# Linear attention in a hybrid encoder layer: pairs by values in quarters of the TensorE array, gate logits as one float32r product

## The chip, the cores and the metric

The kernel runs on one core of a Trainium2 chip, in one launch. The metric is the device time of an execution in microseconds (us). TensorE, VectorE, ScalarE, GpSimd and SyncE are the engines of the core; PE, DVE, ACT, POOL and SP in the profile's lines. PEld is TensorE's weight load.

## The reference, cut to what matters

Two layers (DEPTH = 2) on a sequence of 256 positions of width 2048, all in float32. Each layer projects its input to the operands of three mixers, runs them, gates their outputs with SiLU, and maps them back with one output projection, a residual and a LayerNorm. The change touches the second mixer, a gated linear attention (GLA) with 4 heads, keys of 64 and values of 128, in chunks of 64 positions:

```python
gate_logit = (b_lr @ gate_w + gate_b).astype(jnp.float32)     # (256,16) @ (16,256)
log_g = jax.nn.log_sigmoid(gate_logit) / GATE_TAU
...
def step(state, inp):                                         # one chunk of 64 positions
    qc, kc, vc, gc = inp
    b = jnp.cumsum(gc, axis=1)
    decay = jnp.exp(-jnp.abs(b[:, :, None] - b[:, None, :]))
    attn = jnp.einsum('bihd,bjhd,bijhd->bhij', qc, kc, decay)
    o_intra = jnp.einsum('bhij,bjhv->bihv', attn, vc)
    o_inter = jnp.einsum('bihd,bhdv->bihv', qc * jnp.exp(b), state)
    b_last = b[:, -1]
    k_dec = kc * jnp.exp(b_last[:, None] - b)
    new_state = jnp.exp(b_last)[..., None] * state + jnp.einsum('bjhd,bjhv->bhdv', k_dec, vc)
    return new_state, o_intra + o_inter
...
o_b = o_b * lax.rsqrt(jnp.mean(jnp.square(o_b), axis=-1, keepdims=True) + RMS_EPS) * gla_norm_g
```

`attn` is called the pairs here: one 64 by 64 matrix for each head and chunk. `o_intra` is pairs by values, `o_inter` the product with the state of the chunks before.

## The kernel before, in words

**Main stream.** Nearly all of TensorE's work is the weight products of the projections. A load brings a block of weights (512 KB, or 388 KB in the stage that makes the values, `w388`) into a `raw` tile. ScalarE rounds it to float32r, the high part `wh` (L200), and VectorE subtracts to get the low part `wl` (L207). Three float32r products, high by high, low by high and high by low, stand for one float32 product: `stationary` (weights held in the array, x streams) and `moving` (x held, weights stream) issue them; all matmuls are issued at L77. There are four `raw`, four `wh` and three `wl` buffers, and `take` prepares the high part three loads and the low part two loads ahead.

**Side work.** The mixers are Python generators. After each load that is used, `tick` lets one of at most two active generators, the first in the list that is due, issue its next step; `yield n` says in how many ticks it is due again. The order of TensorE and SyncE is the order in which the program issues; a planner orders the instructions of VectorE, ScalarE and GpSimd by a simulated timeline and by priority, and the weight casts and subtracts have a high priority. Side steps take PSUM banks from a list of four (4 to 7) with `banks(n)` and give them back with `release`, in the order of issue.

**GLA before the change.** `gla_inputs` (L356) loads `gate_w` (16 x 256) into rows 0 to 15 of `gw`, a float32 tile whose other rows are zero. `gla` (L364) then runs these steps:

- The 16 low-rank columns are transposed (L372) and copied by VectorE to rows 0 to 15 of `lrT` (L373). Two ticks later two float32 products of `gw` by `lrT` (L378), 256 columns each, give the gate logits; ScalarE adds the bias (L381).
- The decays are built in visits over levels of distance, and the pairs are put together from masked products (L447, L465, L467), in quarters of the array: 64 rows by 64 columns. `pairs[par]` holds, for heads of parity `par`, four groups g = 2t + b (t: half of the sequence, b: head pair); rows 0 to 63 belong to the even chunk of t, rows 64 to 127 to the odd one.
- The last visit also makes the products for the chunk states (L457), and VectorE sums up the states `st` (L472, L475).
- ScalarE copies the pairs into `attn` (L489), whose tiles have two 64 by 64 blocks on the diagonal and zeros elsewhere (zeroed once, L756). Eight float32 products over the full array (L500) give pairs by values for both chunks of a t at once, and twelve products in quarters (L509) add the state part into the same PSUM region.
- ScalarE copies the two banks to `on` (L512), squares are summed (L516), the RMS factor is applied (L522), and after four more ticks `on` is transposed (L528) and ScalarE writes it, scaled by the norm's gain, to `yraw` (L530).

A float32 product appears in the profile as two matmul rows (two passes), a float32r product as one.

In layer 0 the first attention head (`a_head`) starts while GLA is at its last visit; its first step makes scores in one bank, and VectorE reads them at L542.

Of the kernel before, what the change touches and what calls it, by code (L numbers as in the profile page):

```python
# [8 lines left out]
F32 = mybir.dt.float32  # L9
F32R = mybir.dt.float32r  # L10
I32 = mybir.dt.int32
U8 = mybir.dt.uint8
AF = mybir.ActivationFunctionType
ALU = mybir.AluOpType
AX = mybir.AxisListType

P = 128
D = 2048
T = 256
L = 2  # L20
CH = 64
# [22 lines left out]
def hybrid_trunk_kernel(  # L44
# [7 lines left out]
    pe, dve, act, pool, sp = nc.tensor, nc.vector, nc.scalar, nc.gpsimd, nc.sync  # L52
# [4 lines left out]
    def enter(name, bufs=1, **kw):  # L57
        return ctx.enter_context(tc.tile_pool(name=name, bufs=bufs, **kw))

    cst = enter("cst")  # L60
    per = enter("per")
# [6 lines left out]
    ps = psp.tile([P, 8, 512], F32, name="ps")  # L68
# [3 lines left out]
    def nm(s):  # L72
        uid[0] += 1
        return f"{s}_{uid[0]}"

    def mm(o, l, r, start, stop):
        pe.matmul(o, l, r, start=start, stop=stop, skip_group_check=True)  # L77

    def scratch(shape, dtype=F32):
        return sc.tile(shape, dtype, name=nm("sc"), tag="sc")  # L80

    def small(shape, tag, bufs=1):
        return sm.tile(shape, F32, name=nm(tag), tag=tag, bufs=bufs)
# [30 lines left out]
    def banks(n):  # L114
        while len(free) < n:
            yield 1
        return [free.pop(0) for _ in range(n)]

    def release(*bs):
        free.extend(bs)  # L120
# [183 lines left out]
    def ws_group(l, after=None, first=None):  # L304
        for half in range(2):
            a = pair() if half or first is None else first
            for p in range(4):
                w = take()
                for j in range(4):
                    stationary(a, [v[:, j] for v in w], xq[l][p], j, p == j == 0, p == j == 3)  # L310
                if after:
                    after(half, p)
                if p == 3:
                    v = ps[:, a:a + 2].rearrange("p b (h t) -> p b h t", h=2)
                    yield half * 2, v[:, :, 0], v[:, :, 1]
                tick()
# [39 lines left out]
    def gla_inputs(l):  # L356
        gb = small([P, 2], "gb")
        ng = small([P, 1], "ng")
        pool.dma_start(gw[0:16], gate_w[l])
        pool.dma_start(gb, gate_b[l])  # L360
        pool.dma_start(ng, norm_g[l])
        return gb, ng

    def gla(gb, ng, gq, gk, asv, yraw):  # L364
        gqf = gq.rearrange("p b t -> p (b t)")
        gkf = gk.rearrange("p b t -> p (b t)")
        pairs = [hd.tile([P, 4, CH], F32, name=nm("pairs"), tag=f"pairs{par}") for par in range(2)]
        chunks = lambda a: a.rearrange("p (g c) -> p g c", c=CH)

        pt, = yield from banks(1)  # L370
        for t in range(2):
            pe.transpose(ps[:16, pt, t * P:(t + 1) * P], asv[:, t, 0:16], ident)  # L372
        dve.tensor_copy(lrT[0:16], ps[:16, pt, :T])  # L373
        release(pt)
        yield 2
        pl, = yield from banks(1)
# [44 lines left out]
        qe = hd.tile([P, 512], F32, name=nm("qe"), tag="qe")  # L421
# [6 lines left out]
        st = hd.tile([P, 3, 2, P], F32, name=nm("st"), tag="st")  # L428
        for v, levels in enumerate(VISITS):
            last = v == len(VISITS) - 1  # L430
            if v == 0:
                pt, = yield from banks(1)
# [6 lines left out]
            for i, (lev, (kl, ql)) in enumerate(zip(levels, ready)):  # L439
                o = 256 if last else i * 256  # L440
                for t in range(2):
                    for b in range(2):
                        for half in range(2):
                            for par in range(2):
                                rs = slice(par * 64, par * 64 + 64)
# [3 lines left out]
            if last:  # L449
                kv = (pb[2], pb[1])  # L450
                for c in (0, 1, 2):
                    rs = slice((c % 2) * 64, (c % 2) * 64 + 64)
                    t = c // 2
                    for b in range(2):
                        for par in range(2):
                            h = 2 * b + par
# [3 lines left out]
            for i, lev in enumerate(levels):  # L460
                o = 256 if last else i * 256
# [16 lines left out]
            if not last:  # L478
# [4 lines left out]
                    ready.append(decayed(dd))  # L483
                    yield 1
                yield 1
        for par in range(2):
            for half in range(2):
                hs = slice(half * CH, (half + 1) * CH)
                act.copy(attn[par][hs, :, hs], pairs[par][hs])  # L489
        yield 2  # L490

        on = [scratch([P, 4, P]) for _ in range(2)]
        ms = small([P, 8], "ms")
        sq = small([P, P], "sq")
        po = yield from banks(2)
        for par in range(2):
            for t in range(2):
                for b in range(2):
                    h = 2 * b + par
                    mm(ps[:, po[par], (t * 2 + b) * P:(t * 2 + b + 1) * P], attn[par][:, t * 2 + b],  # L500
                       asv[:, t, 16 + h * P:16 + (h + 1) * P], t == b == 0, False)
        for odd, even in ((1, 2), (3, None)):
            for b in range(2):
                for c in (odd, even):
                    if c is not None:
                        for par in range(2):
                            rs = slice(par * 64, par * 64 + 64)
                            g = (c // 2) * 2 + b
                            mm(ps[(c % 2) * 64:(c % 2) * 64 + 64, po[par], g * P:(g + 1) * P],  # L509
                               qe[rs, b * T + c * CH:b * T + (c + 1) * CH], st[rs, c - 1, b], False, True)  # L510
        for par in range(2):
            act.copy(on[par], ps[:, po[par]].rearrange("p (g c) -> p g c", c=P))  # L512
        release(*po)
        for par in range(2):
            for g in range(4):
                act.activation(sq, on[par][:, g], AF.Square, scale=1.0 / math.sqrt(P),  # L516
# [7 lines left out]
        for par in range(2):  # L524
            pt, = yield from banks(1)
            for t in range(2):
                for b in range(2):
                    pe.transpose(ps[:, pt, b * T + t * P:b * T + (t + 1) * P], on[par][:, t * 2 + b], ident)  # L528
            for b in range(2):
                act.activation(yraw[:, 2 * b + par], ps[:, pt, b * T:(b + 1) * T], AF.Copy, scale=ng[:, 0:1])  # L530
            release(pt)


# [171 lines left out]
    eye = cst.tile([P, CH], F32, name="eye")  # L705
    lnt = cst.tile([P, 2, 16], F32, name="lnt")
    lng = cst.tile([P, P], F32, name="lng")
    gw = cst.tile([P, 256], F32, name="gw")
    lrT = cst.tile([P, 256], F32, name="lrT")
    attn = [per.tile([P, 4, P], F32, name=f"attn{par}") for par in range(2)]  # L710

    plan()
    begin()
# [1 line left out]
    for l in range(L):  # L715
# [7 lines left out]
        for s in range(16):  # L723
            value = s in (0, 1) or (s % 2 == 1 and s < 15)
            p = (s if s < 2 else s // 2 + 1) if value else (s - 2) // 2 if s < 15 else 7
# [22 lines left out]
        yraw = [per.tile([P, 4, T], F32, name=nm("yr"), tag=f"yr{i}") for i in range(4)]  # L748
# [1 line left out]
        gk = hd.tile([P, 2, T], F32, name=nm("gk"), tag="gk")  # L750
        free[:] = []
        if l == 0:
            pool.memset(gw, 0.0)
            pool.memset(lrT, 0.0)
            for a in attn:
                pool.memset(a, 0.0)  # L756
        for i, a, b in ws_group(l, None, 4):
            total(gk if i else gq, a, b, 1.0 if i else 0.125)
        gp = gla_inputs(l)
        if l == 0:  # L760
            sp.dma_start(ident, ident_d)
# [9 lines left out]
        asv = per.tile([P, 2, 1552], F32, name=nm("asv"), tag="asv")  # L771
# [5 lines left out]
        def heads():  # L777
            t = hd.tile([P, 4, T], F32, name=nm("qk"), tag="qk", bufs=4)
            for i, a, b in ws_group(l):
                total(t[:, i:i + 2], a, b)  # L780
            return t
# [13 lines left out]
        load_bias(0)  # L795
        load_bias(1)
        gens = [[gla(*gp, gq, gk, asv, yraw[0])]]
        waiting.extend(gens[0])
        for half in range(2):
            values(2 + half)  # L800
            q, k = heads(), heads()
            gens.append([a_head(half * 4 + h, load_bias, bias, q[:, h], k[:, h], asv, yraw[1 + half][:, h]) for h in range(4)])
            waiting.extend(gens[-1])
        q = [hd.tile([P, 4, T], F32R, name=nm("mq"), tag="qk", bufs=4) for _ in range(2)]
# [158 lines left out]
```

## Time and profile before

| | |
|---|---|
| median of 3 runs | 933.64 us (933.53 to 934.63) |
| profiled execution, own time | 933.71 us |
| its span, first to last instruction | 931.9 us |
| mean granted TensorE clock | 0.998 |
| busy: PE, PEld, DVE, ACT, POOL | 923.4, 812.0, 587.3, 502.0, 16.5 us |
| matmul rows of pairs by values (asv,attn) | 32, two layers of 16 |
| matmul rows of the state part (st,qe) | 48, two layers of 24 |
| matmul rows of the gate logits (lrT,gw) | 8, two layers of 4 |

In a line of a group, the tile left of the arrow is written from those on the right; of a matmul these are the streamed operand first and the one held in the array second. "128*128" or "64*64" is the part of the array that is used, then follow the streamed shape and the count. In a line of the timeline the first number is the start, the second the time from the first start to the last end. Matmuls overlap, so the distance between starts tells what one costs, not its duration.

### The profile page before, as it was taken

The numbers are of one execution on the slowest core, as the hardware profiler recorded it, in microseconds if no ns is written. First come the engines' busy times: TensorE is split into PE (matmuls) and PEld (weight loads), VectorE is DVE, ScalarE is ACT, GpSimd is POOL, SyncE is SP. The second block draws the span as 40 slices with busy tenths as digits, with TensorE's granted clock in tenths as the row PEclk, the third lists the DMA queues.
The fourth block names the chain that finished last, engine by engine and source line by source line (L and its number), as shares of the span: only waits on it lengthen the run. The fifth ranks groups of instructions, "written<-read, shape, count | busy, mean of one in ns | idle before, by whom it ended". The sixth has DMA issues, their size and how long they took to land.

```text
span 931.9 us, 14245 instructions
## 1 busy us (share of the span) xinstructions
PE 923.4 (99%) x5530; PEld 812.0 (87%) x5530; DVE 587.3 (63%) x779; ACT 502.0 (54%) x721; POOL 16.5 (2%) x38
## 2 busy tenths in 40 slices
PE   9999999999999999999999999999999999999997
PEld 6889998998888888888888899889988888888875
DVE  5574487655566666555589645964655666675566
ACT  5564484474456665443468446746644566563440
POOL 1000000000000010000000000000000000100000
PEclk9999999999999999999999999999999999999999
DMA  8867755455545467566666666654655455765642
GB/s 294 283 216 273 209 193 173 147 183 180 196 160 168 171 196 224 192 200 186 203 223 182 187 189 190 201 166 151 196 180 180 164 171 181 220 199 191 198 164 90
DMA packets 58451, 178.72 MB, mean 192 GB/s; under 512 B 6352, under 2 KB 9488, under 8 KB 58128
## 3 DMA queue, kind: packets, MB, share of 16 engines
q1 hardware_dynamic: 56560, 173.05, 57.0%
q0 software_dynamic: 1536, 4.24, 2.0%
q8 instruction: 43, 0.70, 0.3%
q10 hardware_dynamic: 288, 0.52, 0.2%
q14 instruction: 24, 0.20, 0.1%
HBM read 175.70 MB, written 2.10 MB: 191 GB/s over the span
## 4 chain that ended last, share of the span: by engine, by line
PE 96%; DMA 1%; DVE 1%; SPq 0%; issue 0%; ACT 0%; ACTq 0%; DVEq 0%
PE ps L77 95%; DMA room<-w 1%; DMA raw<-w 1%; PE ps L559 1%; DVE wl L207 0%; PE ps L655 0%; PE ps L597 0%; SPq L272 0%; PE ps L528 0%; SPq L267 0%; ACT res L687 0%; ACT wh L200 0%; PE ps L435 0%; DVE res L619 0%; PE ps L372 0%
## 5 line engine op out<-in xcount | busy, mean ns | idle before, releaser
L207 DVE TENSOR_TENSOR wl<-raw,wh 128x1024 fp32r<-128x1024 f32 (+1 forms) x313 | 365.9, 1170 | 273.5 <-PE ps L77 208.2
L200 ACT CAST wh<-raw 128x1024 fp32r<-128x1024 f32 (+1 forms) x313 | 314.7, 1007 | 321.1 <-PE ps L77 226.6
L77 PE MATMUL ps<-x,wh 128*128 128x512 f32 x1408 | 448.8, 400 | 0.1
L77 PEld LDWEIGHTS ps<-x,wl 128*128 128x128 f32 x1408 | 264.4, 188 | 63.2 <-DVE wl L207 1.0
L77 PE MATMUL ps<-wh,x 128*128 128x512 f32 (+1 forms) x1112 | 319.2, 368 | 0.0
L77 PE MATMUL ps<-x,wl 128*128 128x256 f32 x1408 | 277.4, 278 | 0.5 <-DVE wl L207 0.5
L77 PEld LDWEIGHTS ps<-wh,x 128*128 128x128 f32 x1112 | 204.7, 188 | 23.9 <-issue 0.7
L77 PEld LDWEIGHTS ps<-x,wh 128*128 128x128 f32 x1408 | 216.5, 189 | 2.4 <-ACT wh L200 0.5
L77 PE MATMUL ps<-wl,x 128*128 128x512 f32 (+1 forms) x556 | 204.5, 368 | 1.1 <-DVE wl L207 1.1
L77 PEld LDWEIGHTS ps<-wl,x 128*128 128x128 f32 x556 | 104.5, 188 | 14.5 <-DVE wl L207 1.9
L550 ACT ACTIVATE sc<-sc,mx 128x128 f32<-128x128 f32 (+1 forms) x32 | 14.3, 448 | 19.8 <-DVE mx L548 19.8
L338 DVE SCALAR_TENSOR_TENSOR sz<-ps,sz 128x512 f32<-128x512 f32 x24 | 16.4, 689 | 2.3 <-ACT sz L337 0.3
L619 DVE SCALAR_TENSOR_TENSOR res<-res,ps 128x512 f32<-128x512 f32 x16 | 10.9, 683 | 8.0 <-PE ps L77 8.0
L337 ACT ACTIVATE sz<-ps 128x512 f32<-128x512 f32 x24 | 14.2, 593 | 2.0 <-DVE x L342 1.3
L77 PE MATMUL ps<-w,x 128*128 128x512 f32 (+1 forms) x72 | 14.3, 357 | 0.0
L77 PEld LDWEIGHTS ps<-w,x 128*128 128x128 f32 x72 | 12.0, 189 | 2.2
L406 ACT ACTIVATE sc<-sc 128x512 f32<-128x512 f32 x12 | 7.6, 633 | 11.6 <-DVE sc L404 11.6
L831 DVE TENSOR_TENSOR yr<-sz,yr 128x512 f32<-128x512 f32 x16 | 11.0, 687 | 4.2 <-ACT sz L829 4.2
L829 ACT ACTIVATE sz<-sz 128x512 f32<-128x512 f32 x16 | 10.1, 633 | 6.1 <-DVE sz L338 6.0
L77 PE MATMUL ps<-qk,qk 128*128 128x128 f32 (+1 forms) x64 | 13.1, 327 | 0.0
L77 PE MATMUL ps<-sc,asv 128*128 128x256 f32 (+1 forms) x64 | 13.0, 326 | 0.0
L342 DVE TENSOR_TENSOR x<-yr,x 128x512 fp32r<-128x512 f32 x16 | 10.7, 688 | 3.2 <-ACT x L341 3.1
(171 smaller groups left out, 515.1 us busy)
## 6 DMA issues: line engine op xcount, KB each, us to landing
raw<-w SPq DMA_DIRECT2D x252, 512.0 KB, 3.6
raw<-w SPq DMA_DIRECT2D x64, 388.0 KB, 3.1
bias<-relw SPq DMA_DIRECT2D x16, 192.0 KB, 4.0
res<-xT SPq DMA_DIRECT2D x4, 512.0 KB, 6.6
res<-xn SPq DMA_DIRECT2D x1, 2048.0 KB, 8.6
sc<-ln_g POOLq DMA_DIRECT2D x8, 256.0 KB, 4.4
sc<-ln_b POOLq DMA_DIRECT2D x8, 256.0 KB, 6.1
raw<-memT SPq DMA_DIRECT2D x4, 512.0 KB, 4.7
```

Of the source, the lines that this page charges most:

```text
L77: pe.matmul(o, l, r, start=start, stop=stop, skip_group_check=True)
L200: act.copy(d.hi, d.raw)
L207: dve.tensor_tensor(d.lo, d.raw, d.hi.bitcast(F32), op=ALU.subtract)
L337: act.mul(dst, b, scale)
L338: dve.scalar_tensor_tensor(dst, a, scale, dst, op0=ALU.mult, op1=ALU.add)
L342: dve.tensor_tensor(lo, src, hi.bitcast(F32), op=ALU.subtract)
L406: act.activation(dd, dd, AF.Abs)
L550: act.activation(s[:, own[t]], s[:, own[t]], AF.Exp, bias=mx[:, t:t + 1], accum_out=zs[:, t:t + 1])
L559: pe.transpose(ps[:, pt, i * P:(i + 1) * P], s[:, i * P:(i + 1) * P], ident)
L619: dve.scalar_tensor_tensor(r, r, ALPHA, acc, op0=ALU.mult, op1=ALU.add)
L829: act.activation(sz, sz, AF.Silu)
L831: dve.tensor_tensor(yraw[i][:, j:j + 2], sz, yraw[i][:, j:j + 2], op=ALU.mult)
```

## The change

Gate logits: `gw` and `lrT` become float32r tiles. The weights are loaded three times, to rows 0, 32 and 64 of a float32 tile `gws`, and ScalarE rounds each to `gw`; rows 64 to 79 are then replaced by the low part (value minus rounded value). `lrT` gets its high part at rows 0 and 64 (two ScalarE copies from PSUM) and its low part at row 32 (VectorE). One float32r product over the stacked rows gives high by high, high by low and low by high together, with two instructions (one for each b) at the same place as before.

Pairs by values: `attn` with its zeros and its copies is gone. Sixteen products of 64 by 64 quarters take the pairs directly. The product of rows `half` of parity `par` goes to bank `bx[half]`, partitions `(par ^ half) * 64`. The state part goes to two banks of its own, `by[par]`, and no longer adds to the pairs' region. ScalarE copies four quarters to `on`, and VectorE adds the state part: both t for the odd chunks, the second t alone for the even ones (chunk 0 has no state). Four banks are held in place of two. In `on` the halves of parity 1 are swapped, and the last scaled copy to `yraw` puts them back. The generator yields one tick in place of two ahead of the pairs.

```diff
@@ gla_inputs
-        pool.dma_start(gw[0:16], gate_w[l])
+        raw = small([P, 256], "gws")
+        for q in range(3):
+            pool.dma_start(raw[32 * q:32 * q + 16], gate_w[l])
+            act.copy(gw[32 * q:32 * q + 16], raw[32 * q:32 * q + 16])
+        dve.tensor_tensor(gw[64:80], raw[64:80], gw[64:80].bitcast(F32), op=ALU.subtract)
@@ gla
-        dve.tensor_copy(lrT[0:16], ps[:16, pt, :T])
+        for q in (0, 2):
+            act.copy(lrT[32 * q:32 * q + 16], ps[:16, pt, :T])
+        dve.tensor_tensor(lrT[32:48], ps[:16, pt, :T], lrT[0:16].bitcast(F32), op=ALU.subtract)
...
-        for par in range(2):
-            for half in range(2):
-                hs = slice(half * CH, (half + 1) * CH)
-                act.copy(attn[par][hs, :, hs], pairs[par][hs])
-        yield 2
+        yield 1
...
-        po = yield from banks(2)
-        for par in range(2):
-            for t in range(2):
-                for b in range(2):
-                    h = 2 * b + par
-                    mm(ps[:, po[par], (t * 2 + b) * P:(t * 2 + b + 1) * P], attn[par][:, t * 2 + b],
-                       asv[:, t, 16 + h * P:16 + (h + 1) * P], t == b == 0, False)
+        bx = yield from banks(4)
+        by = bx[2:]
+        place = lambda par, half: slice((par ^ half) * CH, (par ^ half) * CH + CH)
+        for g in range(4):
+            t, b = g // 2, g % 2
+            for par in range(2):
+                for half in range(2):
+                    hs = slice(half * CH, (half + 1) * CH)
+                    mm(ps[place(par, half), bx[half], g * P:(g + 1) * P], pairs[par][hs, g],
+                       asv[hs, t, 16 + (2 * b + par) * P:16 + (2 * b + par + 1) * P], True, True)
...
-                            mm(ps[(c % 2) * 64:(c % 2) * 64 + 64, po[par], g * P:(g + 1) * P],
-                               qe[rs, b * T + c * CH:b * T + (c + 1) * CH], st[rs, c - 1, b], False, True)
-        for par in range(2):
-            act.copy(on[par], ps[:, po[par]].rearrange("p (g c) -> p g c", c=P))
-        release(*po)
+                            mm(ps[place(par, c % 2), by[par], g * P:(g + 1) * P],
+                               qe[rs, b * T + c * CH:b * T + (c + 1) * CH], st[rs, c - 1, b], True, True)
+        for half in range(2):
+            for par in range(2):
+                hs = place(par, half)
+                act.copy(on[par][hs], ps[hs, bx[half]].rearrange("p (g c) -> p g c", c=P))
+                g0 = 0 if half else 2
+                o = on[par][hs, g0:]
+                dve.tensor_tensor(o, o, ps[hs, by[par]].rearrange("p (g c) -> p g c", c=P)[:, g0:], op=ALU.add)
+        release(*bx)
...
-            for b in range(2):
-                act.activation(yraw[:, 2 * b + par], ps[:, pt, b * T:(b + 1) * T], AF.Copy, scale=ng[:, 0:1])
+            y = yraw.rearrange("p (b e) (t h c) -> p e h b t c", e=2, t=2, h=2)[:, par]
+            o = ps[:, pt].rearrange("p (b t h c) -> p h b t c", b=2, t=2, h=2)
+            for half in range(2):
+                act.activation(y[:, half], o[:, half ^ par], AF.Copy, scale=ng[:, 0:1])
@@ set-up
-    gw = cst.tile([P, 256], F32, name="gw")
-    lrT = cst.tile([P, 256], F32, name="lrT")
-    attn = [per.tile([P, 4, P], F32, name=f"attn{par}") for par in range(2)]
+    gw = cst.tile([P, 256], F32R, name="gw")
+    lrT = cst.tile([P, 256], F32R, name="lrT")
...
-            for a in attn:
-                pool.memset(a, 0.0)
```

More of the change, by code (lines that the diff above doesn't have):

```diff
@@ L752, in hybrid_trunk_kernel @@
         if l == 0:
-            pool.memset(gw, 0.0)
-            pool.memset(lrT, 0.0)
-            for a in attn:
-                pool.memset(a, 0.0)
+            pool.memset(gw.bitcast(F32), 0.0)
+            pool.memset(lrT.bitcast(F32), 0.0)
         for i, a, b in ws_group(l, None, 4):
```

## The prediction

> **What bounds the kernel now.** I read the page first (busy time, chain), then TensorE's busy time by stretch, then TensorE's timeline around the two places that the diff touches, and last the ScalarE, VectorE and GpSimd rows beside them.
>
> ```profile
> span 931.9 us, 14245 instructions
> PE 923.4 (99%) x5530; PEld 812.0 (87%) x5530; DVE 587.3 (63%) x779; ACT 502.0 (54%) x721; POOL 16.5 (2%) x38
> ...
> PE 96%; DMA 1%; DVE 1%; SPq 0%; issue 0%; ACT 0%; ACTq 0%; DVEq 0%
> ```
> ```profile
> 0.00:14.00 14.00, 11.83 (x37) 8.10 (x38) 6.88 (x14) 7.79 (x13) 3.48 (x12) 1.00 0.80 271
> 14.00:475.00 461.00, 461.00 (x2770) 407.49 (x2770) 287.39 (x372) 249.23 (x351) 6.54 (x13) 1.00 0.62 201
> ...
> 503.00:890.00 387.00, 387.00 (x2418) 345.39 (x2417) 241.93 (x322) 213.35 (x316) 5.33 (x10) 1.00 0.58 184
> ```
> The second fence gives, for each stretch, its length, the busy us of TensorE, its weight loads, VectorE, ScalarE and GpSimd, then granted clock, DMA share and GB/s. Between 14 and 475 and between 503 and 890 us TensorE is never idle, and the chain that ended last is 96% TensorE. Both places of the change, in both layers, lie in these stretches. So a pass taken from TensorE's queue there shortens the run by the pass's spacing (start to start, not its duration, since passes overlap), as long as nothing else becomes late. VectorE and ScalarE work costs nothing until it makes TensorE wait.
>
> **Pairs by values.** These are layer 0 and layer 1 (start, extent, engine, line, operation):
>
> ```profile
> 177.00 0.34 PE L77 MATMUL ps<-wl,x 128*128 128x388 f32 x1
> 177.26 0.69 PE L77 MATMUL ps<-sc,sc 64*64 64x64 f32 x32
> ...
> 180.98 0.82 PE L77 MATMUL ps<-qk,qk 128*128 128x128 f32 x4
> ...
> 183.57 0.34 PE L77 MATMUL ps<-wl,x 128*128 128x388 f32 x1
> 183.75 1.95 PE L77 MATMUL ps<-asv,attn 128*128 128x128 f32 x16
> 185.62 1.09 PE L77 MATMUL ps<-st,qe 64*64 64x128 f32 x24
> 186.65 0.62 PE L77 MATMUL ps<-wh,x 128*128 128x388 f32 x2
> ```
> ```profile
> 641.53 0.34 PE L77 MATMUL ps<-wl,x 128*128 128x388 f32 x1
> 641.71 1.95 PE L77 MATMUL ps<-asv,attn 128*128 128x128 f32 x16
> ...
> 644.60 0.62 PE L77 MATMUL ps<-wh,x 128*128 128x388 f32 x2
> ```
> Eight f32 products of the whole array are 16 passes; they take 183.75 to 185.62 = 1.87 us, 0.11 us each plus the change of array shape at the end. The block from the last weight matmul before (183.57) to the first after (186.65) is 3.08 us; in layer 1, 641.53 to 644.60, 3.07.
>
> The change makes 16 products of 64 rows by 64 columns: 32 passes of 128 values each. What such a pass costs is shown by the state products (st,qe), which stand in quarters already. Three answers of the timeline, each with a window that ends a little later, show how many have started:
>
> ```profile
> 185.62 0.34 PE L77 MATMUL ps<-st,qe 64*64 64x128 f32 x4
> ...
> 185.62 0.45 PE L77 MATMUL ps<-st,qe 64*64 64x128 f32 x8
> ...
> 185.62 0.56 PE L77 MATMUL ps<-st,qe 64*64 64x128 f32 x12
> ...
> 185.78 0.51 PE L77 MATMUL ps<-st,qe 64*64 64x128 f32 x12
> ```
> They start in fours, and each four adds 0.11 us (0.34, 0.45, 0.56): four quarters run at once for the price of one full pass. Only the first four take longer, 185.62 to 185.78 = 0.16 us. The new order within a group g is (rows 0, columns 0), (1,1), (0,1), (1,0): all four quarters, and each row half has a bank of its own, bx[half]. So 32 passes are 8 fours: 0.16 + 7 x 0.11 = 0.93 us. Entering quarters from a weight matmul costs 177.00 to 177.26 = 0.26 us to the first start. The state products then need no change of shape of their own: 1.03 (185.62 to 186.65) less the slow first four, 0.05, is 0.98; their order still spreads over the same quarters. New block: 0.26 + 0.93 + 0.98 = 2.17 us, so 3.08 - 2.17 = 0.91 us saved a layer, 1.82 in all. If only two quarters ran at once it would be 0.26 + 0.16 + 15 x 0.11 + 0.98 = 3.05, a saving of 0.03; I take four, as the nearest row is of the same shape.
>
> The Trainium skill, TensorEngine Tiling (Array Packing), "Restrictions and Gotchas", says that different row tiles cannot write one PSUM bank at the same time. The change keeps to it by the banks above; by that rule alone nothing is lost, and the fours of the trace, whose row halves also have a bank each, agree.
>
> The step's place stays. "yield 1" in place of "yield 2" makes the generator due one tick sooner, but at that tick the first attention head stands ahead of it in the active list (it makes the scores at 180.98), so the pairs come at the tick after that either way. Four banks are free then: a head returns its bank within its step. The last bank in the list is the one that this head's scores used; VectorE reads it 1 us after them, and it is bx[3], which TensorE touches only after the pairs.
>
> **Gate logits.**
>
> ```profile
> 111.35 0.41 DVE L373 COPY lrT<-ps 16x256 f32<-16x256 f32 x1
> ...
> 114.14 0.51 PE L77 MATMUL ps<-wh,x 128*128 128x388 f32 x2
> 114.49 0.34 PE L77 MATMUL ps<-wl,x 128*128 128x388 f32 x1
> 114.67 1.02 PE L77 MATMUL ps<-lrT,gw 128*128 128x256 f32 x4
> ...
> 115.88 0.34 PE L77 MATMUL ps<-wl,x 128*128 128x388 f32 x1
> ```
> ```profile
> 572.63 1.02 PE L77 MATMUL ps<-lrT,gw 128*128 128x256 f32 x4
> ...
> 573.84 0.34 PE L77 MATMUL ps<-wl,x 128*128 128x388 f32 x1
> ...
> 203.11 0.40 PE L77 MATMUL ps<-x,wl 128*128 128x256 f32 x2
> 203.35 0.62 PE L77 MATMUL ps<-x,wh 128*128 128x512 f32 x2
> ```
> Two f32 products of 256 values are four passes; with the two weight matmuls behind them they fill 114.67 to 115.88 = 1.21 us (572.63 to 573.84, the same). A float32r product of 256 values is one pass: the two x,wl from 203.11 to 203.35 are 0.12 us each. Two weight matmuls alone are 0.35 (114.14 to 114.49). New: 2 x 0.12 + 0.35 = 0.59 us; saved 0.62 a layer, 1.24 in all.
>
> The feed of this product grows from one VectorE copy (0.41) to two ScalarE copies out of PSUM and a VectorE subtract. By the copy row these are about 0.4 us each, and the subtract can start after the first: about 0.8 us in all where it was 0.41, with a weight cast (0.84 us) possibly ahead of it in ScalarE's queue. The old copy ended at 111.76, the product starts at 114.67: 2.9 us of cover, so nothing. Without the cover it would cost 0.4 to 1.3 us a layer.
>
> **What the other engines do.**
>
> ```profile
> L338 DVE SCALAR_TENSOR_TENSOR sz<-ps,sz 128x512 f32<-128x512 f32 x24 | 16.4, 689 | 2.3 <-ACT sz L337 0.3
> ...
> L467 DVE COPY_PREDICATED pairs<-lmask,ps 128x256 f32<-128x256 uint8 x24 | 8.8, 437 | 0.2
> ...
> L489 ACT COPY attn<-pairs 64x256 f32<-64x256 f32 x8 | 3.2, 405 | 1.5 <-DVE pairs L467 1.4
> ...
> L512 ACT COPY sc<-ps 128x512 f32<-128x512 f32 x4 | 2.1, 590 | 4.0 <-PE ps L77 4.0
> ```
> ```profile
> 189.12 0.97 DVE L207 TENSOR_TENSOR wl<-raw,wh 128x776 fp32r<-128x776 f32 x1 [3.49 <-ACT sq L516]
> ...
> 193.10 0.49 PE L559 MATMUL ps<-ident,sc 128*128 128x128 f32 x3
> ```
> ScalarE loses four copies of 0.405 and gains two of 0.59 (four quarter copies for two full ones; the 64-row copies above cost no less than full ones, so rows do not matter). VectorE gains two adds of 256 and two of 512 values, by the rows 2 x 0.44 + 2 x 0.69 = 2.3 us, in the 3.49 us in which it stands idle before 189.12. The copies need only the pairs, so they can start before the state products end; the chain from there is about 2.4 us of copies and one last add, 0.7: 3.1 us, against 1.07 for the two copies now. Who waits: the squares behind it, a low part of weights on VectorE (189.12 to 190.09; it is for the load after next, and a load here is 12 weight matmuls at 0.18 us, 183.57 to 183.75, so 2 x 2.1 us on, near 193), and the next head's bank request at 193.10, 6.4 us after the block ends. All have 3 us or more. Cost zero; uncovered it is 2 us a layer.
>
> **The start.**
>
> ```profile
> 4.96 6.13 DMA raw<-w
> 11.11 1.06 ACT wh L200
> ...
> 12.19 1.24 DVE wl L207
> ...
> 13.47 6.64 PE ps L77 x33
> ```
> ```profile
> L278 ACT CAST x<-res 128x256 fp32r<-128x256 f32 x4 | 1.6, 405 | 2.3 <-DMA res<-memT 2.3
> ```
> Here the chain is not TensorE. Three gate loads of 16 KB stand where one was, two 0.5 us memsets leave GpSimd, and ScalarE gets three copies (0.4 each, by the 256-value cast), VectorE a subtract (0.4). The planner may put them between the first casts. ScalarE waits for DMA between most of those, so most is covered; a copy that lands between 11.11 and 13.47 delays all that follows. 32 KB more at 271 GB/s are 0.12 us. I take 0.1, between 0 and 1.6 (all four on the chain). In layer 1 the same copies only follow the layer 0 product, far ahead of use: 0.
>
> **Sum.** 933.71 is the profiled execution's own time (span 931.9 and 1.8 around it), 0.07 above the median of 933.64. -1.82 - 1.24 + 0.1 = -2.96, so 930.75 by that execution and 930.7 by the median: -0.3%. Below 0.2%, 1.87 us, a measurement of this kernel cannot tell it from no change.
>
> **The rivals.**
> - *The start takes it back.* Two to four of the gate copies stand in the chain before 13.47: +0.8 to +1.6, so 931.4 to 932.2. For: ScalarE's queue is in order, and these copies wait for GpSimd's slow loads. Against: the chain there hangs on a DMA that lands at 11.11, and ScalarE has gaps before. 12%, half of it still faster by 1.87.
> - *Only two quarters at once*, so only the gate counts: -0.06 - 1.24 + 0.1, 932.4. For: the two column halves of one row half now write one bank, in an order that crosses the array. Against: the fours above. 8%.
> - *A late low part.* VectorE's adds wait for ScalarE's copies and hold a weight subtract, and TensorE loses 0.5 to 1 us a layer: 931.7 to 932.7. It needs 3 us of delay. 5%.
> - *Slower: the banks.* The generator now holds all four side banks until the last add. If the next head asks for one within 3.1 us of the block's end, TensorE, in order, stands with all weight matmuls behind it. Fully open twice, 6.2 us: 933.64 - 2.96 + 6.2 = 936.9. It decides only if the copies start 3.3 us late, as the request comes 6.4 us behind (193.10). 4%. The Trainium skill, TensorEngine Tiling, "PSUM Bottleneck", warns of just this, that tiling does not speed up emptying PSUM; here TensorE has other work meanwhile, so the warning bears only on this rival.
>
> The forecast itself: 71%. **Range** 930.0 to 932.4: the low end has the passes' own spread (0.02 us on each of some forty steps), the high end takes in the start rival and the two quarters. Chances: faster 0.71 + 0.06, same the rest of the rivals but the last, 0.19, slower 0.04.
>
> **What would show it.** In the changed profile: 32 passes named asv,pairs at 64*64 in each layer, 0.9 us from their start to st,qe; two lrT,gw passes a layer with 0.12 between them; the block 2.2 us long; no new row of TensorE waiting for VectorE's adds or ScalarE's copies; TensorE's steady work starting within 0.2 us of 13.47. I am wrong if the pairs take more than 1.5 us, if TensorE waits at 114 or 193, or if the start moves by half a microsecond.

## The result, and the profile after

The changed kernel takes 930.29 us (median of 8 runs, 929.74 to 933.56); the kernel before took 934.63 on the same chip (8 runs, 933.53 to 935.19). The ratio is 0.9959, with a 95% interval of 0.9948 to 0.9970: 2.8 to 4.9 us less. The profiled execution took 930.37 us where that of before took 933.71, so 3.3 us less. The forecast was 3.0 less by the profiled execution and a time of 930.7.

The page of the changed kernel, the lines that answer to those of before:

```profile
span 928.6 us, 14327 instructions
PE 920.9 (99%) x5558; PEld 808.5 (87%) x5558; DVE 592.7 (64%) x789; ACT 503.7 (54%) x727; POOL 17.6 (2%) x40
...
PE 96%; DMA 1%; DVE 1%; SPq 1%; issue 0%; ACT 0%; ACTq 0%; DVEq 0%
```

TensorE is still the bound, with 28 more rows and 2.5 us less busy time. Its timeline at the pairs in layer 0 and layer 1 of the changed kernel (start, extent, operation, count):

```profile
183.43 0.34 PE L77 MATMUL ps<-wl,x 128*128 128x388 f32 x1
183.69 1.10 PE L77 MATMUL ps<-asv,pairs 64*64 64x128 f32 x32
184.62 1.05 PE L77 MATMUL ps<-st,qe 64*64 64x128 f32 x24
185.60 0.62 PE L77 MATMUL ps<-wh,x 128*128 128x388 f32 x2
...
639.79 0.34 PE L77 MATMUL ps<-wl,x 128*128 128x388 f32 x1
640.05 1.10 PE L77 MATMUL ps<-asv,pairs 64*64 64x128 f32 x32
...
641.96 0.62 PE L77 MATMUL ps<-wh,x 128*128 128x388 f32 x2
```

The block from the last weight matmul before to the first after is 2.17 us in both layers (183.43 to 185.60, 639.79 to 641.96). The 32 quarter passes take 183.69 to 184.62 = 0.93 us. At the gate logits of the two layers:

```profile
115.15 0.40 PE L77 MATMUL ps<-lrT,gw 128*128 128x256 f32 x2
115.39 0.52 PE L77 MATMUL ps<-wh,x 128*128 128x388 f32 x2
115.74 0.34 PE L77 MATMUL ps<-wl,x 128*128 128x388 f32 x1
...
571.46 0.40 PE L77 MATMUL ps<-lrT,gw 128*128 128x256 f32 x2
...
572.06 0.34 PE L77 MATMUL ps<-wl,x 128*128 128x388 f32 x1
```

Two passes, 0.12 us each (115.15 to 115.39), and the two weight matmuls behind them: 115.15 to 115.74 = 0.59 us, 571.46 to 572.06 = 0.60. Next, the start of the run (chain of waits) and its end (timeline):

```profile
4.96 6.56 DMA raw<-w
...
11.54 1.06 ACT wh L200
...
13.90 6.24 PE ps L77 x31
```
```profile
898.84 0.50 PE L77 MATMUL ps<-wl,x 128*128 128x512 f32 x1 [0.50 <-DVE wl L207]
...
922.14 1.98 PE L77 MATMUL ps<-gbrow,row 2*128 2x512 f32 x4 [0.34 <-ACT row L696]
```
The kernel before, same places at the end:
```profile
901.68 0.50 PE L77 MATMUL ps<-wl,x 128*128 128x512 f32 x1 [0.71 <-DVE wl L207]
...
924.97 1.98 PE L77 MATMUL ps<-gbrow,row 2*128 2x512 f32 x4 [0.34 <-ACT row L683]
```

With these rows and those of the prediction, the difference between the two profiled executions can be followed through the run:

| mark | before | after | after minus before |
|---|---|---|---|
| first of the steady weight matmuls | 13.47 | 13.90 | +0.43 |
| second weight matmul after the gate, layer 0 (wl) | 115.88 | 115.74 | -0.14 |
| first weight matmul after the pairs, layer 0 | 186.65 | 185.60 | -1.05 |
| same after the gate, layer 1 | 573.84 | 572.06 | -1.78 |
| same after the pairs, layer 1 | 644.60 | 641.96 | -2.64 |
| first matmul after the wait for the last weights | 901.68 | 898.84 | -2.84 |
| last group of matmuls | 924.97 | 922.14 | -2.83 |
| end of the span | 931.9 | 928.6 | -3.3 |

The start gives back 0.43; each gate takes about 0.6 and each pairs block 0.9. TensorE's wait near 475 us, between the two layers, is 0.16 shorter (0.35 before, 0.19 after), the one at 900 is 0.2 shorter (0.71 and 0.50), and 0.5 us goes after the last group of matmuls. The last three lie where the change does nothing. From the first steady matmul to the end of the last one, without these two waits, TensorE takes 912.4 us before and 909.5 after: 2.9 us less.

### The profile page after: what moved, and what is told of

The parts are those of the page before. It is cut to its first block, busy times and chain, and to the rows that moved or that the text cites. A ratio compares the mean times of both kernels' runs of the same rounds, so it can differ in the third digit from the quotient of the medians.

```text
span 928.6 us, 14327 instructions
## 1 busy us (share of the span) xinstructions
PE 920.9 (99%) x5558; PEld 808.5 (87%) x5558; DVE 592.7 (64%) x789; ACT 503.7 (54%) x727; POOL 17.6 (2%) x40
## 4 chain that ended last, share of the span: by engine, by line
PE 96%; DMA 1%; DVE 1%; SPq 1%; issue 0%; ACT 0%; ACTq 0%; DVEq 0%
PE ps L77 95%; DMA raw<-w 1%; DMA room<-w 1%; DVE wl L207 1%; PE ps L572 1%; PE ps L668 0%; PE ps L610 0%; SPq L272 0%; PE ps L539 0%; SPq L267 0%; ACT res L700 0%; DVE w L207 0%; ACT wh L200 0%; PE ps L441 0%; SPq L179 0%
## 5 line engine op out<-in xcount | busy, mean ns | idle before, releaser
L200 ACT CAST wh<-raw 128x1024 fp32r<-128x1024 f32 (+1 forms) x313 | 314.8, 1007 | 327.4 <-PE ps L77 228.7
```

The source lines that it names most:

```text
L200: act.copy(d.hi, d.raw)
```

## The experiments

**One part at a time.** The first run has the pairs as changed and the gate lines as before, the second the gate as changed and the pairs as before (its raw weights lie in a buffer of another tile).

```diff
 # e1: the changed kernel
...
-            act.copy(gw[32 * q:32 * q + 16], raw[32 * q:32 * q + 16])
+        pool.dma_start(gw[0:16], gate_w[l])
...
-        for q in (0, 2):
-            act.copy(lrT[32 * q:32 * q + 16], ps[:16, pt, :T])
...
+        dve.tensor_copy(lrT[0:16], ps[:16, pt, :T])
```


> The pairs and the sums as changed, the gate logits as before. Passes theory: the block from the last weight matmul before the pairs to the first after is 2.17 us in both layers, the gate product stays 1.21 us with its two neighbours, and TensorE's steady work starts at 13.47 as before, since the gate copies at the start are gone: 1.8 us below before by the profile. Rival, only the gate pays and the pairs' gain is given back by the sums: within 0.3 us of before.

```diff
 # e2: the kernel before, with the gate lines of the change, and
+        raw = hd.tile([P, 384], F32, name=nm("bias"), tag="bias", bufs=3)[:, :256]
```


> The gate logits as changed (the raw weights lie in a bias buffer, for room), the pairs as before. Passes theory: two passes with 0.12 us between them, the stretch 1.21 to 0.59 us in each layer, so 1.24 us less, and the start 0.4 us later as in the changed kernel (13.90): 0.8 us below before. Rival, the start's 0.4 us is chance of that one execution: start at 13.47 and 1.2 us below before.

Pairs alone: 931.86 us, ratio to before 0.9974 (0.9964 to 0.9984), so 1.5 to 3.4 us less. Gate alone: 931.60, 0.9978 (0.9969 to 0.9987), so 1.2 to 2.9 less. The timeline of the first, and of the second:

```profile
183.77 0.34 PE L77 MATMUL ps<-wl,x 128*128 128x388 f32 x1
184.04 1.10 PE L77 MATMUL ps<-asv,pairs 64*64 64x128 f32 x32
...
185.94 0.45 PE L77 MATMUL ps<-wh,x 128*128 128x388 f32 x1
```
```profile
115.10 0.40 PE L77 MATMUL ps<-lrT,gw 128*128 128x256 f32 x2
...
115.69 0.34 PE L77 MATMUL ps<-wl,x 128*128 128x388 f32 x1
```

The block is 2.17 us (183.77 to 185.94) and the gate 0.59 (115.10 to 115.69), each without the other part. In TensorE's queue both parts have the sizes forecast. The times show more than that: the pairs run is 2.4 us below before by its ratio and 2.5 by its profiled execution (931.19), where 1.8 was expected; the gate run 2.1 by its ratio, where 0.8 was expected and lies outside the interval, and 1.0 by its profiled execution (932.74). Steady work starts at 13.70 in the pairs run, not at the 13.47 expected, and at 13.93 in the gate run. These two alone do not show that the gate copies move it: runs further down that leave the lines of the first 14 us as in the changed kernel start anywhere from 13.56 to 13.92.

**The order of the quarters.** The same sixteen products, but now four in a row, eight passes, stay in one quarter.

```diff
-        for g in range(4):
-            t, b = g // 2, g % 2
+        for half in range(2):
+            hs = slice(half * CH, (half + 1) * CH)
             for par in range(2):
-                for half in range(2):
-                    hs = slice(half * CH, (half + 1) * CH)
+                for g in range(4):
+                    t, b = g // 2, g % 2
```


> The changed kernel with the same sixteen products in another order: four in a row in the same quarter. Fours theory (four quarters run at once only if neighbours in the queue name different quarters): passes follow one another at 0.11 us, 32 x 0.11 = 3.5 us in place of 0.93, so the block grows by 2.6 us a layer and the run by 5.2 us over the changed kernel, to about 935.5. Rival, the queue sorts them out and order does not matter: the block stays near 2.2 us.

932.79 us, ratio to before 0.9986 (0.9976 to 0.9995), 2.5 us above the changed kernel. The timeline, and below it two answers whose windows end 0.4 us apart:

```profile
183.22 0.34 PE L77 MATMUL ps<-wl,x 128*128 128x388 f32 x1
183.48 2.24 PE L77 MATMUL ps<-asv,pairs 64*64 64x128 f32 x29
185.46 0.32 PE L77 MATMUL ps<-st,qe 64*64 64x128 f32 x1
...
185.78 0.27 PE L77 MATMUL ps<-asv,pairs 64*64 64x128 f32 x1
...
186.85 0.62 PE L77 MATMUL ps<-wh,x 128*128 128x388 f32 x2
```
```profile
183.48 0.81 PE L77 MATMUL ps<-asv,pairs 64*64 64x128 f32 x6
...
183.48 1.14 PE L77 MATMUL ps<-asv,pairs 64*64 64x128 f32 x12
```

The block is 3.63 us (183.22 to 186.85), 1.46 longer than in the order of the change and 0.55 longer than the old full-array block of 3.08: in this order the quarters lose. So the fours come from the order of issue: neighbours must name different quarters. But the queue does better than one pass at a time: six passes start in those 0.4 us, where one at a time would be fewer than four. Followed start by start, the eight passes of one quarter are 0.11 us apart, 0.16 after the first, as if they stood alone; what overlaps is the next quarter. The first passes of the four quarters start at 183.48, 183.97, 184.47 and 184.96, 0.49 us apart, where eight passes one after another take 0.9. The first state product, in another quarter again, starts at 185.46, before the last three of the 32 passes (the last at 185.78), though it was issued behind them. The expected 2.6 us more a layer was too much, since it took the whole queue to be serial.

**The start.** The gate loads are issued by SyncE at their place in the program, away from the start; or they stay on GpSimd, but behind two memsets of 0.5 us, as long as those that the change removed.

```diff
-            pool.dma_start(raw[32 * q:32 * q + 16], gate_w[l])
+            sp.dma_start(raw[32 * q:32 * q + 16], gate_w[l])
```
```diff
             pool.memset(lrT.bitcast(F32), 0.0)
+            for _ in range(2):
+                pool.memset(scratch([P, 512]), 0.0)
```


> The changed kernel with the three gate loads issued by SyncE at their place in the program (in layer 0 after the key and query weights) in place of GpSimd at the start, so loads and casts leave the first 14 us. Start theory: the first big weight load lands near 11.1 and steady work starts at 13.47, 0.4 us below the changed kernel. Rival, the landing at 11.54 varies by itself: no difference from the changed kernel beyond 0.2 us, and a start anywhere between 13.4 and 13.9.

> The changed kernel with two GpSimd memsets of 0.5 us ahead of the gate loads, as the zeroing of the old tiles stood there before. Theory, the loads that GpSimd issues a microsecond sooner delay the first big weight load: first x,wl matmul back near 13.5, 0.4 us below the changed kernel. Rival, the three loads and casts themselves, or something else at the start: 13.9 again and no difference.

Loads later: 931.03 us, ratio to before 0.9967 (0.9955 to 0.9980). Behind memsets: 931.09, 0.9965 (0.9953 to 0.9977). Neither is told apart from the changed kernel. The chain at the start, in that order:

```profile
12.23 1.05 ACT wh L200
...
14.59 5.57 PE ps L77 x27
```
```profile
13.70 6.48 PE ps L77 x32
```

Without any gate load or copy in the first 14 us the first big weight load still lands at 12.2, later than in any other run, and TensorE's steady work starts at 14.59, 1.1 us later than expected. So the start theory falls: the landing can be late without the gate's loads. The copies are not out of it in every run. In the changed kernel ScalarE waits for the load; in the gate run, and in the same way behind the memsets, a gate copy (L362) stands right ahead of the cast of that load (L200). ScalarE's rows of the changed kernel, and the chain of the gate run:

```profile
11.54 1.05 ACT L200 CAST wh<-raw 128x1024 fp32r<-128x1024 f32 x1 [0.72 <-DMA raw<-w]
```
```profile
11.14 0.40 ACT gw L362
...
11.56 1.06 ACT wh L200
```

**Second executions** of the two kernels, unchanged:

> The kernel before once more, one look. Theory that single executions differ at four places that the change does not touch (the landing of the first big weight load, the memory load near 475, the last weight loads near 900, the time after the last matmul): between the first x,wl matmul and the last matmul, less the stalls at 475 and 900, it is 912.1 us again, while start, stalls and tail differ from the first execution by some tenths each. Rival, the start belongs to the kernel: first x,wl at 13.47 again.

> The changed kernel once more, one look. Same theory: 909.2 us between first x,wl and last matmul less the two stalls, as in its first execution, and a start other than 13.90. Rival, the start belongs to the kernel: 13.90 again.

Before again: 934.60 us, span 932.8; changed again: 930.34, span 928.6. Steady work starts at

```profile
13.53 6.48 PE ps L77 x32
```
```profile
13.91 6.27 PE ps L77 x31
```

So each of the two kernels repeats its own start in these two executions (13.47 and 13.53, 13.90 and 13.91), against the theory that single executions scatter. Four other runs leave the lines that run in the first 14 us as they are in the changed kernel and differ only later (the order of the quarters above, and the three runs below). They started at 13.79, 13.56, 13.92 and 13.69. What in a kernel sets it stays open. The changed kernel repeats its span, and its 909.5 us from the first steady matmul to the end of the last without the two waits. The one before is 0.9 us longer this time: 0.06 at the start, 0.4 in the two waits (1.48 in place of 1.06), and 0.4 in between (912.8 in place of 912.4), where the theory expected the same again. The first execution of before was thus a quick one among its runs, and this is part of why the times show more than the profiles (3.8 by the ratio, 4.3 by the medians, against 3.3).

**How much cover the sums have.** Each quarter copy and each add is done twice, then four times, with the same values.

```diff
+                for again in range(2):      # range(4) in the other
-                act.copy(on[par][hs], ps[hs, bx[half]].rearrange("p (g c) -> p g c", c=P))
+                    act.copy(on[par][hs], ps[hs, bx[half]].rearrange("p (g c) -> p g c", c=P))
...
```


> The changed kernel with each quarter copy and each VectorE add done twice over (the same values), so that emptying the four banks takes about 5.5 us after the pairs in place of 3. Cover theory: the next head asks for a bank 6.4 us after the block and the low part behind the adds has 3 us or so, so at most 0.3 us more a layer; the net TensorE time stays 909.2 to 909.8. Rival, the banks or the adds are on the edge already: 2 us more a layer, 913.

> The same with each copy and add done four times: emptying takes about 10 us. Cover theory: now past the cover of 6.4 us, so TensorE waits for a bank or a low part in both layers, 2 to 5 us each, and the rows of the wait name VectorE's adds or a weight subtract; 4 to 10 us above the changed kernel. Rival, the planner moves the extra work aside and nothing waits: within 1 us of the changed kernel.

Twice: 940.88 us, ratio to before 1.0069 (1.0053 to 1.0086), so 10.6 above the changed kernel's 930.29; four times: 957.27, 1.0249 (1.0234 to 1.0264). Both expectations were far off. (The net TensorE time they speak of is that from the first steady matmul to the last, without the waits near 475 and 900.) Who waited in layer 0, twice and four times:

```profile
PE ps L540 <- DVE sc L534: 3.3, 1, 3.3
```
```profile
PE ps L573 <- ACT sc L521: 5.5, 1, 5.5
...
PE ps L540 <- DVE sc L534: 4.3, 1, 4.3
```

L540 are the transposes of the normed output, L534 its scaling by the RMS factor, L573 a head's transposes into one of the four banks, L521 the quarter copies. At four times the bank is late, the mechanism of the slower rival. At twice it is not; what waits there is GLA's own next step. The cover of that step is seen in the changed kernel:

```profile
184.85 2.27 ACT L520 COPY sc<-ps 64x512 f32<-64x512 f32 x4 [0.25 <-PE ps L77]
```
```profile
185.77 0.41 DVE L523 TENSOR_TENSOR sc<-sc,ps 64x256 f32<-64x256 f32 x1 [0.29 <-PE ps L77]
186.55 1.74 DVE L523 TENSOR_TENSOR sc<-sc,ps 64x512 f32<-64x512 f32 x3 [0.36 <-ACT sc L520]
...
195.63 1.29 DVE L533 TENSOR_TENSOR sc<-sc,rr 128x512 f32<-128x512 f32 x2
```
```profile
200.08 1.03 PE L539 MATMUL ps<-ident,sc 128*128 128x128 f32 x8
```

Adds done at 188.29 (186.55 + 1.74), scaling done at 196.92, transposes at 200.08: 3.2 us. The same two in the kernel before:

```profile
196.08 1.29 DVE L522 TENSOR_TENSOR sc<-sc,rr 128x512 f32<-128x512 f32 x2
```
```profile
201.12 1.03 PE L528 MATMUL ps<-ident,sc 128*128 128x128 f32 x8
```

There it was 201.12 less 197.37, 3.7 us. Twice the copies and adds delay the scaling by more than their own 4.4 us on the two engines together: between the first quarter copy and the RMS factor ScalarE now takes five weight casts, where it took two in the changed kernel, and VectorE's weight subtracts stand between the adds. The scaling starts at

```profile
202.38 1.28 DVE L534 TENSOR_TENSOR sc<-sc,rr 128x512 f32<-128x512 f32 x2
```

6.75 us later than in the changed kernel. And the wait of TensorE costs more than its length. The busy time by stretch, with the granted clock as the third number from the end:

```profile
185.00:199.00 14.00, 14.00 (x86) 13.47 (x83) 10.10 (x15) 13.06 (x33) 0.00 (x0) 1.00 0.61 182
199.00:204.00 5.00, 1.71 (x10) 1.42 (x9) 3.04 (x7) 2.41 (x3) 0.00 (x0) 0.81 0.60 187
204.00:212.00 8.00, 8.00 (x36) 7.07 (x35) 3.47 (x8) 4.99 (x10) 0.54 (x1) 0.69 0.24 76
```

The granted clock is 0.69 on the mean in the 8 us from 204. In shorter stretches of the same trace it is 1.00 up to 202, 0.50 from 202.25 to 208.75, and 1.00 again from 209; in layer 1, after a wait as long, it is 0.50 from 666.5 to 669.5. The Trainium skill, TensorE: Matmul & The Clock Gate, Part 1, says that the gate falls to half after an idle window of about 3.4 us and rises again after as long a busy one. The halving agrees; the lengths agree only in part: in layer 0 the clock falls 2.2 us after the last matmul ended (199.83) and stays at half for 6.8 us, in layer 1 it falls 0.8 us after TensorE was at work again and stays there for 3.4. An estimate from these figures: the two waits cost 6.6 us and the half clock, while TensorE worked, half of 5.8 and half of 3.4, 4.6 more; 11.2 in all, where the profiled spans differ by 11.6 (940.2 and 928.6).

To see whether that step is all, it was put later:

```diff
         dve.tensor_tensor(on[par], on[par], rr[:, par * 4:par * 4 + 4].unsqueeze(2).to_broadcast([P, 4, P]), op=ALU.mult)
-        yield 4
+        yield 7
```


> Copies and adds twice over, as in the run that lost 5 us a layer, but the step that transposes the normed output comes seven ticks after the one before it in place of four. Theory: what waited was neither a bank nor a low part but these transposes, whose operand was done 3.3 us late, and the idle time then halved the granted clock for some us; three ticks (some 8 us) more cover it, so the waits of 3.34 us at the transposes and the lower clock go, and net TensorE time is 909.2 to 909.8, the run about 930.5. Rival, the extra work makes weights late as well: some of the 10.5 us stays, 933 or more.

930.63 us, ratio to before 0.9955 (0.9940 to 0.9971): all 10 us are gone, with the doubled copies and adds still in. The same stretches:

```profile
199.00:204.00 5.00, 5.00 (x32) 4.42 (x31) 3.25 (x8) 3.33 (x4) 0.00 (x0) 1.00 0.49 163
204.00:212.00 8.00, 8.00 (x52) 7.12 (x51) 5.77 (x10) 6.69 (x14) 0.00 (x0) 1.00 0.60 201
```

TensorE waits nowhere between 185 and 215 us. So neither banks nor weights were late at twice, only the transposes.

## Why the prediction was right, point by point

- *The bound.* TensorE without a gap in the stretches of the change, so passes taken out shorten the run: shown by the marks, where the savings are still there at the last matmul.
- *Pairs by values.* 0.91 us a layer forecast. The block went from 3.08 to 2.17 in layer 0 and from 3.07 to 2.17 in layer 1, the quarter passes 0.93 as worked out from the fours of the state products. The order run shows that the fours make the gain, since the same 32 passes in another order lose to the old block. The rival of two quarters at once is out for this order.
- *Gate logits.* 0.62 a layer forecast, 0.62 and 0.61 measured.
- *The start.* Taken as 0.1 between 0 and 1.6, measured 0.43: outside the 0.2 us that the prediction named as its sign, short of the half microsecond that it named as being wrong. In the changed kernel none of the gate copies stands in the chain; the load itself lands 0.43 later. In the gate run and behind the memsets two copies do, as the start rival had it, and without any load or copy there the start is the latest of all. This term was sized by a cause that does not act in the changed kernel; what moves the landing is open.
- *The rest.* The sum gave -2.96 and the last group of matmuls stands at -2.83, but that they are so near is partly luck: the start took 0.33 more than forecast, and the waits near 475 and 900, for which the sum had no term, gave 0.37. Without start and waits it is 2.9 measured against 3.06 forecast, or 3.3 with the second execution of before. The other 0.5 us of the profiles lies behind the last group of matmuls, and some 0.5 more of the times in the scatter of before's executions. The prediction had no term for either. The first of them goes with the gate lines: in the three profiled executions with the old ones (before, twice, and pairs alone) the span ends 6.8 to 7.0 us after the start of that group, in the nine with the changed ones 6.5 to 6.6. Why it does is open.
- *Cost zero for the sums.* Right, but the guard was named wrongly. The forecast's 3 us for "the squares behind it" did not follow them to the transposes four ticks on, which have 3.2 us left; before it was 3.7. I had named the bank and the low part as what would become late first, and the doubled run shows it to be the transposes, at a price of 10.6 us. The slower rival was real at four times the work, not at one.

## What to carry to other kernels

When TensorE has no gap, cost an edit by the distance between starts, and look for an operation of the same shape already in the trace: the state products gave the price of the quarters to 0.01 us. Small products in quarters ran four at once here when neighbours in the queue named different quarters, and at most two at once with eight passes of one quarter in a row, so write the loop so that neighbours differ. When work is moved to engines off the path, follow its result to the next TensorE step that reads it, not only to the buffer that it holds, and remember that a wait long enough to lower the clock costs more than itself.

## What the runs showed of the hardware that was not expected

- The order of issue held within a quarter, not between quarters: with eight passes of one quarter in a row these were 0.11 us apart, but the next quarter began 0.49 us after the one before, and a state product started 0.32 us ahead of a pass of the pairs that was issued before it (185.46 and 185.78). The block was 3.63 us, where one after another at 0.11 would have given about 4.8 (0.26 + 32 x 0.11 + 0.98).
- Doubling 4.4 us of copies and adds (2.27 on ScalarE, 2.15 on VectorE) in each of two layers cost 10.6 us, and after a wait of 3.3 us the granted clock was at half for 6.8 us in one layer and 3.4 in the other.
- The landing of the first big weight load moved between 11.1 and 12.2 us with edits that do not touch it, and the end of the span behind the last group of matmuls by 0.5 us with the gate lines.
